# The cumulative sum of the newest gates queued behind the state, and the filling of even slots moved ahead of the output, in a hybrid encoder block

## The chip, the cores and the metric

The kernel runs on one core of a Trainium2 chip. The metric is the device time in microseconds of one execution. Three runs of the kernel before took 1623.01 to 1624.67 us, median 1623.91.

A core has a matrix engine (TensorE, PE in the profile), a vector engine (VectorE, DVE), a scalar engine for activation functions (ScalarE, ACT), an engine that issues most DMAs (SyncE, SP), and GpSimd (POOL), which is hardly used here. Matmuls write to PSUM; DVE and ACT read it out into SBUF. Each engine works through its own queue in order and waits on semaphores for the others.

## The reference

One layer of an encoder over 1024 tokens of width 1024, in float32. The part that matters here is the gated linear attention with 4 heads, keys of 128, values of 256, in both directions:

```
h = RMSNorm(x);  q, k, v, r, gate codes, ... = split(h @ W_in)
log_g = max(log_sigmoid(codes @ up + bias) / 16, -0.5)
b = cumsum(log_g) within a chunk                 # _gla_direction
q_dec = q * exp(b); k_inv = k * exp(-b); k_tail = k * exp(b_last - b)
scores = where(mask, q_dec @ k_inv^T, 0)
o = scores @ v + q_dec @ state
state = exp(b_last) * state + k_tail^T v         # from chunk to chunk
```

The forward direction includes the diagonal, the backward one does not. The two outputs are added, normed per head, gated, and projected. Beside it stands a windowed softmax attention (8 query heads, 2 key heads, window 128), then the merge of the two with an output projection, and a SwiGLU feed-forward.

## The kernel before, in words

Each float32 operand of a matmul is split into a high part (fp32r) made by ACT and a rest made by DVE, and `mm3` (L75) multiplies high by high, high by low and low by high. So every loaded weight of 128x512 costs one ACT copy (`wh`, L67) and one DVE subtraction (`wl`, L69).

The kernel is written with a layer that orders the instructions of DVE, ACT and SP by itself, from the order in the program and its own estimate of when each is ready. Only for PE the written order is kept (`tc.manual_schedule`). Once ordered, each queue is fixed.

The linear attention works in chunks of 128 tokens, NC = 8 for each of NH = 4 heads, 32 in all, as a pipeline over slots `t`. In slot `t` these stages are due (the loop that fills `at` and `behind`):

- `g_gates` for a pair of chunks, in even slots 0 to 30: a matmul of the gate codes into PSUM (`z`), ACT Exp (L419), DVE min (L420), ACT Ln (L421), the DVE scan over 128x512 that makes the cumulative sum (L422), and two small DVE operations for `sm`, the sums at the ends of half chunks (L425, L426). All of it lives in one tile `G`, which has a single buffer.
- `g_decays` (L437 to L444), traced as the last thing of the same even slot: DVE differences, two ACT Exp (L440, L441), and two DVE products with k and q (L443, L444). `g_parts` one slot later splits the results for the matmuls (L451 to L456).
- `g_scores`, three slots after the gates, in odd slots: v is loaded and split (L467, L468), the keys turned on PE and split (L475, L476), the scores computed, read out by ACT into `sp` (L483), masked by DVE (L484) and split into `sh` and `sl` (L487, L488).
- `g_out` for chunk n in slot n + 4, so in every slot from 4 to 35: six matmuls `kv` for the state in both directions; DVE makes the new state `pf` (L502; L506 in a head's first chunk); ACT copies the backward half to `kb` (L504); ACT makes `th`, the high part of the decayed state (L514), and DVE the rest `tl` (L515). Then PE does the output `o`: three matmuls of `sh`, `sl` with v, and three of q with the `th` and `tl` that the *previous* `g_out` made. ACT copies `o` out of PSUM into `ob` (L522).
- `g_back_out`, from slot 12 on in every slot: the backward output (three matmuls with `thb`, `tlb`, L533 and L534), added to `ob` by DVE (L544), and the step of the backward state (`kb`, L536). `g_turn`, twice in each odd slot from 15 on: two transposes and a copy.

Even slots of the steady state thus have the stages gates, back output, output; odd slots have turn, turn, back output, output, scores. Between the stages `slot` (L274) puts filling: matmuls of 128x512 of the other projections, `share(GF, t)` of them in a slot (34 up to slot 7, 21 up to 23, 18 up to 35, then 11). Of `n` fillings and `s` stages, `n * (j + 1) // s` are done after stage `j`, so an equal share stands behind each stage, the last one included. Stages are separate items of the list `work`, and `g_decays` is added to the last of them. `x_sums` adds one or two DVE operations a slot (L576, L581).

All small PSUM tiles of these stages (`z`, `kv`, `o`, the back output, the turned tiles, the scores) share four buffers with the tag `ch`; a tile waits until the one four before it has been read. The tiles `vh`, `kth`, `sh` and their like have one buffer, `th`, `tl` and `pf` two.

Of the kernel before, what the change touches and what calls it, by code (L numbers as in the profile page):

```python
# [8 lines left out]
F32 = mybir.dt.float32  # L9
FR = mybir.dt.float32r  # L10
U32 = mybir.dt.uint32
AF = mybir.ActivationFunctionType
ALU = mybir.AluOpType
# [6 lines left out]
NC = 8  # L20
# [3 lines left out]
GF = ((8, 34), (24, 21), (36, 18), (1 << 30, 11))  # L24
# [6 lines left out]
def body(tc, i, out):  # L31
    nc = tc.nc
    with ExitStack() as root:
# [233 lines left out]
        def share(plan, t):  # L267
            return next(n for end, n in plan if t < end)

        def need(key):  # L270
            while key not in scr:
                fill(12)

        def slot(stages, n):  # L274

            stages = [f for f in stages if f]
            done = 0
            if not stages:
                fill(n)
            for j, f in enumerate(stages):  # L280
                f()
                t = n * (j + 1) // len(stages)
                fill(t - done)
                done = t

# [109 lines left out]
            pass  # L395

        gla = {}

        def g_gates(hd, c):


            pr = Chunk()
            for j in range(2):
                a = gla[hd, c + j] = Chunk()
                a.pr, a.j, a.t = pr, j, slice(j * P, (j + 1) * P)
            s, co = c // 4, (c % 4) * P
            for nme in ("q", "k"):
                need((f"{nme}{hd}", s))
            qk = gtile("qk", (P, 2, 256))
            nc.sync.dma_start(out=qk[:, 0], in_=scr[f"q{hd}", s][:, co:co + 256])  # L410
            nc.sync.dma_start(out=qk[:, 1], in_=scr[f"k{hd}", s][:, co:co + 256])
            z = chtile((P, 2, 256))
            for d in range(2):
                mm(z[:, d], upS[:, d, hd * P:(hd + 1) * P], lrS[:, c * P:(c + 2) * P], True, True)
            G = gtile("G", (P, 4, 2, P), bufs=1)
            Gt = G.rearrange("p a j t -> p a (j t)")
            Gf = G.rearrange("p a j t -> p (a j t)")
            cs, e, csf, ef = G[:, 0:2], G[:, 2:4], Gf[:, 0:512], Gf[:, 512:1024]
            nc.scalar.activation(ef, z.rearrange("p d t -> p (d t)"), AF.Exp, scale=-1.0)  # L419
            nc.vector.tensor_scalar(ef, ef, float(np.expm1(8.0)), None, op0=ALU.min)  # L420
            nc.scalar.activation(ef, ef, AF.Ln, bias=ones[:, 0:1])  # L421
            nc.vector.tensor_tensor_scan(csf, mask.rearrange("p c t -> p (c t)"), ef, 0.0, op0=ALU.mult, op1=ALU.add)  # L422

            pr.sm = gtile("sm", (P, 2, 2, 2), bufs=16)
            nc.vector.tensor_scalar(pr.sm, cs[:, :, :, 63:128:64], -1.0 / 16, None, op0=ALU.mult)  # L425
            nc.vector.tensor_tensor(pr.sm[:, :, :, 1], pr.sm[:, :, :, 1], pr.sm[:, :, :, 0], op=ALU.subtract)  # L426

            pr.qk, pr.G = qk, G

        def g_decays(hd, c):  # L430
            pr = gla[hd, c].pr
            qk, G = pr.qk, pr.G
            Gt = G.rearrange("p a j t -> p a (j t)")
            Gf = G.rearrange("p a j t -> p (a j t)")
            cs, e, csf, ef = G[:, 0:2], G[:, 2:4], Gf[:, 0:512], Gf[:, 512:1024]
            late = bass.AP(Gf.tensor, Gf.offset, [list(Gf.ap[0]), [255, 2], [P, 2], [1, P]])
            nc.vector.tensor_tensor(e, late, cs[:, :, :, 63:64].to_broadcast([P, 2, 2, P]), op=ALU.subtract)  # L437
            nc.vector.tensor_scalar(e[:, 1, :, 0:1], cs[:, 1, :, 63:64], -1.0, None, op0=ALU.mult)

            nc.scalar.activation(csf, ef, AF.Exp, scale=-1.0 / 16)  # L440
            nc.scalar.activation(ef, ef, AF.Exp, scale=1.0 / 16)  # L441
            pr.en = gtile("en", (P, 2, 256))
            nc.vector.tensor_tensor(pr.en, Gt[:, 1:3], qk[:, 1:2].to_broadcast([P, 2, 256]), op=ALU.mult)  # L443
            nc.vector.tensor_tensor(Gt[:, 0:4:3], Gt[:, 0:4:3], qk[:, 0:1].to_broadcast([P, 2, 256]), op=ALU.mult)  # L444
# [48 lines left out]
        def g_out(hd, c):  # L493

            a = gla[hd, c]
            kv = chtile((P, 2, 256))
            for d in range(2):
                mm3(kv[:, d], a.kth[:, d], a.ktl[:, d], a.vh, a.vl, True, True)
            a.pf = gtile("pf")
            if c:  # L500
                pf, dec, th, tl = a.before
                nc.vector.scalar_tensor_tensor(a.pf, pf, dec[:, 0:1], kv[:, 0], op0=ALU.mult, op1=ALU.add)  # L502
                a.kb = gtile(f"kb{c}", bufs=2 if c < 5 else 1)
                nc.scalar.copy(a.kb, kv[:, 1])  # L504
            else:
                nc.vector.tensor_copy(a.pf, kv[:, 0])  # L506
                a.kb = None
            if c < NC - 1:
                n = gla[hd, c + 1]
                dec2 = gtile("dec", (P, 1))  # L510
                nc.scalar.activation(dec2, n.pr.sm[:, 0, n.j, 0:1], AF.Exp, bias=a.pr.sm[:, 0, a.j, 1:2])
                th2 = gtile("th", dt=FR)
                tl2 = gtile("tl", dt=FR)
                nc.scalar.activation(th2, a.pf, AF.Copy, scale=dec2[:, 0:1])  # L514
                nc.vector.scalar_tensor_tensor(tl2, a.pf, dec2[:, 0:1], th2.bitcast(F32), op0=ALU.mult, op1=ALU.subtract)  # L515
                n.before = a.pf, dec2, th2, tl2
            o = chtile((P, 256))
            mm3(o, a.sh, a.sl, a.vh, a.vl, True, c == 0)
            if c:
                mm3(o, a.pr.q2[0][:, 0, a.t], a.pr.q2[0][:, 1, a.t], th, tl, False, True)  # L520
            a.ob = gtile(f"ob{c}", bufs=2 if c < 5 else 1)
            nc.scalar.copy(a.ob, o)  # L522

        def g_back(hd, c):

# [84 lines left out]
        at, behind = {}, {}  # L610
        last = 0
        for n in range(NH * NC):
            hd, c = divmod(n, NC)
            cb = hd * NC + NC + 4 + (NC - 1 - c)
            tt = cb + c % 2 + 2
            for j, (t, f) in enumerate(((n, g_gates), (n + 3, g_scores), (n + 4, g_out),
# [3 lines left out]
                last = max(last, t)  # L620
# [4 lines left out]
        with tc.manual_schedule(engines={mybir.EngineType.PE}):  # L625
            fill(36)
            for t in range(last + 1):
                work = [[at[t, j]] for j in (0, 5, 4, 3, 2, 1) if (t, j) in at]
                if t in behind:
                    work = work or [[]]  # L630
                    work[-1].append(behind[t])
                slot([lambda v=v: [f(*a) for f, *a in v] for v in work], share(GF, t))
                if t:
                    next(sums, None)
        glas.close()
# [186 lines left out]
        for n in range(2 * KT):  # L822
            t, g = divmod(n, 2)
# [9 lines left out]
        order = (prep, a_rope, a_scores, a_turn, k_turn, a_out, a_probs)  # L833
# [165 lines left out]
        with tc.manual_schedule(engines={mybir.EngineType.PE}):  # L999
# [15 lines left out]
            for j in range(0, len(PAIRS), 2):  # L1015
# [4 lines left out]
                v = [pair_T3(f) for f in two]  # L1020
# [561 lines left out]
```

## Time and profile before

| | |
|---|---|
| median of three runs | 1623.91 us |
| the profiled execution | 1624.31 us |
| its span, first to last instruction | 1622.5 us |
| granted TensorE clock | 1.00 throughout |
| busy share of DVE and ACT over the span | 75% and 56% |
| first Exp of the gates (L419) to last copy of a turn (L565) | 49.1 to 368.4 us |

The profile is one execution. Times are in microseconds from the span's start. A row of the timeline has the start, the duration, the engine, the line of the kernel, the operation, the tile written and the tiles read, and in brackets how long the engine sat idle before it and what ended that. Matmuls are pipelined: the duration of one is longer than the step to the next, so PE's pace is read from starts. In the names, `ch` is a small PSUM tile, `mm` one of the filling's; `ch<-vh,kth` is a product for the state, `ch<-vh,sh` one of scores with v, `ch<-th,q2f` one of q with the state.

### The profile page before, as it was taken

The page shows a single profiled execution, that of the slowest core. Times are in us where ns is not written, and L with a number is a line of the kernel's source. Part 1 is how long each engine was busy: PE and PEld are TensorE (multiplying, and loading weights), DVE is VectorE, ACT ScalarE, POOL GpSimd, SP SyncE. Part 2 cuts the span into 40 slices and gives each one's busy share as a digit, 9 for nine tenths or more (in the row PEclk, how much of TensorE's full clock was granted, in tenths as well). Part 3 has the DMA queues.
Part 4 walks back from the last instruction along what each step waited for, and adds up shares of the span by engine and source line. Part 5 has one row for each costly group of instructions (what it writes and reads, how often), then busy time and mean ns, then how long its engine had stood idle before and what let it go on. Part 6 is the DMA issues. An engine that isn't in the chain of part 4 may idle for free.

```text
span 1622.5 us, 23392 instructions
## 1 busy us (share of the span) xinstructions
PE 1611.6 (99%) x7644; PEld 1341.5 (83%) x7644; DVE 1223.9 (75%) x2315; ACT 915.0 (56%) x1883; POOL 0.2 (0%) x4
## 2 busy tenths in 40 slices
PE   9999999999999999999999999999999999999999
PEld 7888888888888888888888888888888888888887
DVE  8568888845999777876855878677777888789655
ACT  7456777873999745445732547754444444354442
POOL 0000000000000000000000000000000000000000
PEclk9999999999999999999999999999999999999999
DMA  8855757878554487878842656643435564695433
GB/s 279 295 180 194 252 172 256 274 264 284 176 162 143 129 268 253 270 242 263 282 126 89 192 192 214 196 141 124 136 121 177 170 219 146 207 328 189 149 98 117
DMA packets 196362, 323.25 MB, mean 199 GB/s; under 512 B 22318, under 2 KB 47790, under 8 KB 196240
## 3 DMA queue, kind: packets, MB, share of 16 engines
q1 hardware_dynamic: 196240, 321.76, 60.8%
q8 instruction: 60, 0.98, 0.2%
q14 instruction: 62, 0.51, 0.1%
HBM read 216.29 MB, written 105.38 MB: 198 GB/s over the span
## 4 chain that ended last, share of the span: by engine, by line
PE 89%; DVE 4%; ACT 3%; DMA 2%; issue 1%; SPq 0%; DVEq 0%; ACTq 0%
PE mm L73 20%; PE mm L877 10%; PE mm L879 10%; PE mm L878 10%; PE mm L1421 7%; PE ch L73 7%; PE ch L1421 6%; PE ch L878 5%; PE ch L879 5%; PE ch L877 5%; PE mm L246 3%; PE ch L783 1%; DMA kvr<-skv 1%; DMA st<-in_xT_dram 1%; DVE wl L69 0%
## 5 line engine op out<-in xcount | busy, mean ns | idle before, releaser
L856 ACT ACTIVATE wh<-ws 128x512 fp32r<-128x512 f32 x164 | 102.9, 629 | 152.5 <-PE mm L878 81.0
L73 PE MATMUL mm<-wh,xh 128*128 128x512 f32 x320 | 127.1, 397 | 0.0
L73 PE MATMUL mm<-wh,xl 128*128 128x512 f32 x320 | 127.1, 397 | 0.0
L73 PE MATMUL mm<-wl,xh 128*128 128x512 f32 x320 | 126.6, 395 | 0.0
L857 DVE TENSOR_TENSOR wl<-ws,wh 128x512 fp32r<-128x512 f32 x164 | 112.2, 686 | 14.0 <-ACT wh L856 13.5
L67 ACT ACTIVATE wh<-wr 128x512 fp32r<-128x512 f32 x118 | 73.5, 627 | 53.0 <-PE mm L73 21.3
L69 DVE TENSOR_TENSOR wl<-wr,wh 128x512 fp32r<-128x512 f32 x118 | 80.8, 686 | 25.2 <-ACT wh L67 22.8
L856 ACT ACTIVATE wh<-a 128x512 fp32r<-128x512 f32 x66 | 41.6, 632 | 89.1 <-PE ch L1421 42.3
L856 ACT ACTIVATE wh<-wr 128x512 fp32r<-128x512 f32 x76 | 47.8, 631 | 58.1 <-PE mm L878 17.6
L857 DVE TENSOR_TENSOR wl<-a,wh 128x512 fp32r<-128x512 f32 x66 | 45.5, 690 | 39.7 <-ACT wh L856 39.3
L1421 PE MATMUL mm<-hh,wl 128*128 128x512 f32 x176 | 68.6, 390 | 0.0
L1421 PE MATMUL mm<-hl,wh 128*128 128x512 f32 x176 | 68.5, 389 | 0.0
L1421 PE MATMUL mm<-hh,wh 128*128 128x512 f32 x176 | 68.5, 389 | 0.0
L73 PEld LDWEIGHTS mm<-wl,xh 128*128 128x128 f32 x320 | 60.2, 188 | 9.8
L73 PEld LDWEIGHTS mm<-wh,xl 128*128 128x128 f32 x320 | 60.2, 188 | 9.6
L73 PEld LDWEIGHTS mm<-wh,xh 128*128 128x128 f32 x320 | 60.3, 188 | 9.1 <-DVE st L141 0.2
L857 DVE TENSOR_TENSOR wl<-wr,wh 128x512 fp32r<-128x512 f32 x76 | 52.0, 685 | 7.8 <-ACT wh L856 7.1
L870 DVE TENSOR_TENSOR ws<-wr,wr 128x512 f32<-128x512 f32 x80 | 54.5, 687 | 4.3 <-DMA wr<-in_w_f_dram 1.7
L1388 DVE TENSOR_TENSOR hl<-hr,hh 128x512 fp32r<-128x512 f32 x77 | 52.8, 686 | 5.7 <-ACT hh L1387 5.4
L1387 ACT ACTIVATE hh<-hr 128x512 fp32r<-128x512 f32 x77 | 47.7, 619 | 9.0 <-DMA hr<-B 5.1
L1421 PE MATMUL ch<-hh,wh 128*128 128x512 f32 x132 | 51.3, 389 | 0.0
L1421 PE MATMUL ch<-hl,wh 128*128 128x512 f32 x132 | 51.3, 389 | 0.0
(454 smaller groups left out, 4984.5 us busy)
## 6 DMA issues: line engine op xcount, KB each, us to landing
wr<-in_w_fi_dram SPq DMA_DIRECT2D x110, 256.0 KB, 3.9
wr<-in_w_f_dram SPq DMA_DIRECT2D x100, 256.0 KB, 3.7
wh<-wh SPq DMA_DIRECT2D x80, 256.0 KB, 3.1
wl<-wl SPq DMA_DIRECT2D x80, 256.0 KB, 3.1
B<-c SPq DMA_DIRECT2D x44, 256.0 KB, 2.1
T<-st SPq DMA_DIRECT2D x44, 256.0 KB, 2.9
a<-in_w_fo_dram SPq DMA_DIRECT2D x44, 256.0 KB, 5.3
hr<-T SPq DMA_DIRECT2D x44, 256.0 KB, 2.7
```

The costliest lines, as they stand in the source:

```text
L67: nc.scalar.activation(h, raw, AF.Copy)
L69: nc.vector.tensor_tensor(l, raw, h.bitcast(F32), op=ALU.subtract)
L73: nc.tensor.matmul(o, a, b, start=start, stop=stop)
L246: nc.tensor.matmul(Y[q], w[:, c], x, start=f0, stop=f1, skip_group_check=True)
L856: nc.scalar.activation(h, src, AF.Copy)
L857: nc.vector.tensor_tensor(l, src, h.bitcast(F32), op=ALU.subtract)
L870: nc.vector.tensor_tensor(t, x, y, op=op)
L877: nc.tensor.matmul(o, h[:, c], x[kk][0], start=start and kk == 0, stop=False, skip_group_check=True)
L878: nc.tensor.matmul(o, h[:, c], x[kk][1], start=False, stop=False, skip_group_check=True)
L879: nc.tensor.matmul(o, l[:, c], x[kk][0], start=False, stop=kk == nk - 1, skip_group_check=True)
L1388: nc.vector.tensor_tensor(l, r, h.bitcast(F32), op=ALU.subtract)
L1421: nc.tensor.matmul(ys[m], a[:, c], b, start=f0, stop=f1, skip_group_check=True)
```

## The change

Three functions are touched.

1. The scan and the two `sm` operations move from the end of `g_gates` to the start of what was `g_decays`, now `g_sums`. `g_decays` traces all of `g_sums` in `tc.issue_after(v)` for each `v` in the list `state`: every instruction in the block is queued behind `v` on `v`'s engine. `state` holds `th`'s ACT instruction and `tl`'s DVE instruction of the last `g_out` that made them. In an even slot `g_out` is traced just ahead of `g_decays`, so these are the same slot's. Before slot 4 the list is empty.
2. `g_out` notes these two instructions.
3. `slot` takes a flag. Where it is false and there is more than one stage, the `n` fillings are spread behind all stages but the last, none behind the last. It is false in even slots that have an output (4 to 34).

The number of instructions and of fillings in a slot stays.

```diff
-        def slot(stages, n):
+        def slot(stages, n, last=True):
...
-                t = n * (j + 1) // len(stages)
+                t = n * (j + 1) // len(stages) if last or len(stages) == 1 else n * min(j + 1, len(stages) - 1) // (len(stages) - 1)
...
         gla = {}
+        state = []
...
             nc.scalar.activation(ef, ef, AF.Ln, bias=ones[:, 0:1])
-            nc.vector.tensor_tensor_scan(csf, mask.rearrange("p c t -> p (c t)"), ef, 0.0, op0=ALU.mult, op1=ALU.add)
-
-            pr.sm = gtile("sm", (P, 2, 2, 2), bufs=16)
-            nc.vector.tensor_scalar(pr.sm, cs[:, :, :, 63:128:64], -1.0 / 16, None, op0=ALU.mult)
-            nc.vector.tensor_tensor(pr.sm[:, :, :, 1], pr.sm[:, :, :, 1], pr.sm[:, :, :, 0], op=ALU.subtract)
-
             pr.qk, pr.G = qk, G
 
         def g_decays(hd, c):
-            pr = gla[hd, c].pr
+            with ExitStack() as order:
+                for v in state:
+                    order.enter_context(tc.issue_after(v.ins))
+                g_sums(gla[hd, c].pr)
+
+        def g_sums(pr):
             qk, G = pr.qk, pr.G
...
+            nc.vector.tensor_tensor_scan(csf, mask.rearrange("p c t -> p (c t)"), ef, 0.0, op0=ALU.mult, op1=ALU.add)
+
+            pr.sm = gtile("sm", (P, 2, 2, 2), bufs=16)
+            nc.vector.tensor_scalar(pr.sm, cs[:, :, :, 63:128:64], -1.0 / 16, None, op0=ALU.mult)
+            nc.vector.tensor_tensor(pr.sm[:, :, :, 1], pr.sm[:, :, :, 1], pr.sm[:, :, :, 0], op=ALU.subtract)
+
             late = bass.AP(Gf.tensor, Gf.offset, [list(Gf.ap[0]), [255, 2], [P, 2], [1, P]])
...
-                nc.scalar.activation(th2, a.pf, AF.Copy, scale=dec2[:, 0:1])
-                nc.vector.scalar_tensor_tensor(tl2, a.pf, dec2[:, 0:1], th2.bitcast(F32), op0=ALU.mult, op1=ALU.subtract)
+                v1 = nc.scalar.activation(th2, a.pf, AF.Copy, scale=dec2[:, 0:1])
+                v2 = nc.vector.scalar_tensor_tensor(tl2, a.pf, dec2[:, 0:1], th2.bitcast(F32), op0=ALU.mult, op1=ALU.subtract)
...
             nc.scalar.copy(a.ob, o)
+            if c < NC - 1:
+                state[:] = v1, v2
...
-                slot([lambda v=v: [f(*a) for f, *a in v] for v in work], share(GF, t))
+                slot([lambda v=v: [f(*a) for f, *a in v] for v in work], share(GF, t), t % 2 == 1 or (t, 2) not in at)
```

More of the change, by code (lines that the diff above doesn't have):

```diff
@@ L421, in g_gates, with g_decays @@
             nc.scalar.activation(ef, ef, AF.Ln, bias=ones[:, 0:1])
+            pr.qk, pr.G = qk, G
+        def g_decays(hd, c):
+            with ExitStack() as order:
[3 more added lines that the diff above has]
+        def g_sums(pr):
+            qk, G = pr.qk, pr.G
+            Gt = G.rearrange("p a j t -> p a (j t)")
+            Gf = G.rearrange("p a j t -> p (a j t)")
+            cs, e, csf, ef = G[:, 0:2], G[:, 2:4], Gf[:, 0:512], Gf[:, 512:1024]
             nc.vector.tensor_tensor_scan(csf, mask.rearrange("p c t -> p (c t)"), ef, 0.0, op0=ALU.mult, op1=ALU.add)
```

6 lines of the change are left out of this document (removed).

## The prediction

> **What bounds the kernel now.** I read the page first: TensorE (PE) is busy all the time, and the chain that ended last is PE for 89% of the span. So only two things can move the time: idle of PE that goes, and idle that comes.
>
> ```profile
> PE 1611.6 (99%) x7644; PEld 1341.5 (83%) x7644; DVE 1223.9 (75%) x2315; ACT 915.0 (56%) x1883; POOL 0.2 (0%) x4
> ```
>
> Next came the table of busy time by stretch. Its columns are the stretch, its length, then busy time and instruction count of PE, weight loads (PEld), DVE and ACT. The slots of the linear attention fill the first quarter of the span. Its slots 4 to 11 lie in the first row below; slots 28 to 31 lie in the rows from 270 to 315.
>
> ```profile
> 75.00:145.00 70.00, 70.00 (x381) 60.38 (x380) 50.13 (x100) 35.75 (x79) 0.00 (x0) 1.00 0.58 191
> 270.00:285.00 15.00, 15.00 (x91) 13.13 (x90) 13.30 (x33) 11.45 (x35) 0.00 (x0) 1.00 0.74 229
> 285.00:300.00 15.00, 13.66 (x83) 11.43 (x82) 13.15 (x32) 12.83 (x34) 0.00 (x0) 1.00 0.86 295
> 300.00:315.00 15.00, 15.00 (x93) 13.16 (x92) 14.33 (x35) 12.87 (x37) 0.00 (x0) 1.00 0.84 283
> 740.00:1100.00 360.00, 359.38 (x1585) 297.20 (x1584) 259.37 (x414) 196.99 (x338) 0.00 (x0) 1.00 0.59 186
> ```
>
> Three things are to be seen. The early slots have no idle PE at all (70.00 of 70.00). The last pairs of slots lose some, and there DVE is nearly full (14.33 of 15). And a 512-wide matmul takes PE 360/1585 = 0.23 us from start to start where nothing waits, although its row says 0.39; so a wait has to be read from the starts. The view of the waits of PE names what it waited for in the attention (total, times, longest):
>
> ```profile
> PE ch L73 <- ACT ob L522: 1.4, 2, 1.1
> PE ch L73 <- DVE sh L487: 0.8, 2, 0.6
> PE ch L73 <- DVE sl L488: 0.2, 1, 0.2
> ```
>
> That is 2.4 us of idle in five places. PE's timeline at these five places, from start to start:
>
> ```profile
> 217.40 0.28 PE L73 MATMUL ch<-vl,sh 128*128 128x256 f32 x1
> 217.84 0.39 PE L73 MATMUL ch<-vh,sl 128*128 128x256 f32 x1 [0.16 <-DVE sl L488]
> ...
> 224.03 0.28 PE L73 MATMUL ch<-vh,ktl 128*128 128x256 f32 x1
> 224.64 0.38 PE L73 MATMUL ch<-vh,sh 128*128 128x256 f32 x1 [0.33 <-ACT ob L522]
> ...
> 285.73 0.28 PE L73 MATMUL ch<-vh,ktl 128*128 128x256 f32 x1
> 286.27 0.36 PE L73 MATMUL ch<-vh,sh 128*128 128x256 f32 x1 [0.26 <-DVE sh L487]
> 286.86 0.40 PE L73 MATMUL mm<-wh,xl 128*128 128x512 f32 x1
> ...
> 291.14 0.40 PE L73 MATMUL mm<-wh,xl 128*128 128x512 f32 x1
> 292.62 0.39 PE L73 MATMUL ch<-vh,kth 128*128 128x256 f32 x1 [1.08 <-ACT ob L522]
> ...
> 315.22 0.28 PE L73 MATMUL ch<-vh,ktl 128*128 128x256 f32 x1
> 316.07 0.36 PE L73 MATMUL ch<-vh,sh 128*128 128x256 f32 x1 [0.57 <-DVE sh L487]
> ```
>
> The normal step of a 256-wide matmul is 0.12 us (next fence: 106.31 to 106.43). Above the normal step the five places lose 0.32, 0.49, 0.42, 1.25 and 0.73 us, 3.2 together. Behind a wait the next matmuls are slow too: from 286.27 to 286.86 three of them take 0.59 where 0.36 is normal, 0.23 more. With 0.1 to 0.23 behind four of them, I count **3.9 us** as all that this stage can give back. Against the span that is 0.24%.
>
> What makes them wait is order on DVE and ACT. The longest one, on those engines' timelines (slot 28, an even one):
>
> ```profile
> 287.71 1.22 DVE L422 TENSOR_TENSOR_SCAN G<-mask,G 128x512 f32<-128x512 f32 x1 [0.79 <-ACT G L421]
> 289.05 0.68 DVE L437 TENSOR_TENSOR G<-G 128x512 f32<-128x512 f32 x1
> 289.73 0.42 DVE L506 COPY pf<-ch 128x256 f32<-128x256 f32 x1
> ...
> 290.18 0.51 ACT L514 ACTIVATE th<-pf,dec 128x256 fp32r<-128x256 f32 x1 [1.41 <-DVE pf L506]
> 292.20 0.36 ACT L522 COPY ob<-ch 128x256 f32<-128x256 f32 x1
> ```
>
> The products for the state ended at about 286 (285.73 + 0.28), yet `pf` starts at 289.73, because the newest gates' scan and L437 were put in front of it. ACT stood idle 1.41 us for `pf`; the copy of the output out of PSUM (L522) is behind that in ACT's queue, and PE needed the PSUM buffer that it frees.
>
> **The change part by part.**
>
> *The scan behind the state.* No instruction is added; the scan, the two `sm` operations, and the whole of `g_decays` (DVE L437 to L444, ACT L440 and L441) come behind `th` and `tl` of the same slot's `g_out`. That takes 1.22 + 0.68 us and the small ones, about 2 us, from in front of `pf`. Queued behind the new order are only these operations themselves. Their readers are `g_parts` one slot later and `g_scores` three slots later, and the next pair's Exp into the single buffer G two slots later, so being some 3 us late costs nothing by my count. What hides this is DVE's free time late in the odd slot and early in the even slot; without it the readers are late, see the second rival. No DMA is moved by this and no SP queue passed. The next late thing is `pf` itself, behind the state's matmuls.
>
> *No filling behind the output in even slots.* The number of dense matmuls in a slot stays, so no matmul is added. In slots of three stages a third of the filling (7 of 21, 6 of 18, at 0.23 us each: 1.6 or 1.4 us) goes from behind the output to in front of it. So the scores (`sh`, `sl`) of the slot before have that much more time before an even `g_out` needs them; three of the five waits are such, and none had more than 0.73 us. The other two (`ob`) wait behind `pf` in an even slot. All five lie in the reach of one half or the other: **minus 3.9 us**, and I take half of it, 2 us, as the weak end.
>
> What it costs: the next `g_out`, in the odd slot, comes sooner. From slot 14 on two turns, a back output and 8 to 12 fillings lie between. Slot 14 of before:
>
> ```profile
> 170.08 0.28 PE L73 MATMUL ch<-vh,ktl 128*128 128x256 f32 x1
> ...
> 177.19 0.28 PE L73 MATMUL ch<-th,q2f 128*128 128x256 f32 x1
> ```
>
> From the last product for the state to the first matmul that reads it are 7.1 us, and 7.1 - 1.6 = 5.5 after the change. Slots 4, 6, 8 and 10 are another matter. They have two stages (gates; output), so all filling goes in front of the output; and the odd slots behind them begin with their own `g_out`, as no turn and no back output exists yet. There **two outputs now stand back to back**. How long does PE need from the one's last product to the matmul that reads its `tl`, and how long does the state need? Rows of slot 6 and slot 8 (PE, DVE, ACT):
>
> ```profile
> 106.31 0.28 PE L73 MATMUL ch<-vh,ktl 128*128 128x256 f32 x1
> 106.43 0.28 PE L73 MATMUL ch<-vh,sh 128*128 128x256 f32 x1
> ...
> 106.63 0.48 DVE L502 SCALAR_TENSOR_TENSOR pf<-pf,dec,ch 128x256 f32<-128x256 f32 x1 [0.41 <-PE ch L73]
> ...
> 126.38 0.47 DVE L502 SCALAR_TENSOR_TENSOR pf<-pf,dec,ch 128x256 f32<-128x256 f32 x1
> 126.89 0.37 ACT L504 COPY kb<-ch 128x256 f32<-128x256 f32 x1 [0.34 <-DVE pf L502]
> 127.15 0.51 ACT L514 ACTIVATE th<-pf,dec 128x256 fp32r<-128x256 f32 x1
> 127.70 0.48 DVE L515 SCALAR_TENSOR_TENSOR tl<-pf,dec,th 128x256 fp32r<-128x256 f32 x1 [0.77 <-ACT th L514]
> ```
>
> PE: six matmuls of the first output, six products, three of `sh`, then `th` and `tl`: the 17th matmul, 17 x 0.12 = 2.04 us (14 x 0.12 = 1.68 in slot 4, whose output has three matmuls). The state with free engines: 106.63 - 106.31 = 0.32 to the start of `pf`, then 127.70 + 0.48 - 126.38 = 1.80 to the end of `tl`, 2.12 us. So it is late by 0.08 us at the least, and with the slow restart 0.1 to 0.3. The other end is slot 10, where the scan and a weight's split stood in the way:
>
> ```profile
> 139.70 0.28 PE L73 MATMUL ch<-vh,ktl 128*128 128x256 f32 x1
> ...
> 143.12 0.48 DVE L515 SCALAR_TENSOR_TENSOR tl<-pf,dec,th 128x256 fp32r<-128x256 f32 x1
> ```
>
> 143.60 - 139.70 = 3.9 us, late by 1.86, with the restart 2.1. The lower end is the nearer row, since the scan is now behind the state; but DVE and ACT still take a split of a weight now and then (0.69 us on DVE, by the page's row), just ahead of `pf` or `th`:
>
> ```profile
> L69 DVE TENSOR_TENSOR wl<-wr,wh 128x512 fp32r<-128x512 f32 x118 | 80.8, 686 | 25.2 <-ACT wh L67 22.8
> ```
>
> I take **0.6 us a pair, four pairs: plus 2.4 us**, ends 0.4 and 8.4. A gain is excluded there: no idle exists in that stretch. The sum of filling before slot 4 and behind slot 36 is untouched.
>
> Sum: -3.9 + 2.4 + 0.2 for a wait somewhere that I don't see = **-1.3 us**. The profiled execution took 1624.31 us (span 1622.5, 1.8 around it), 0.4 above the median 1623.91; it would become 1623.0, and the median **1622.6**.
>
> A rule to weigh: the PE column of the stretch from 285 to 300 loses 15 - 13.66 = 1.34 us, whereas the starts say 0.42 + 0.23 + 1.25 + 0.1 = 2.0. The Trainium skill, Perfetto Trace Analysis, section Identifying the Most-Contended Engine, says that matmul busy time is a poor measure and that the busy share of weight loads is a good one. By that share this stretch does 11.43 where the one before does 13.13 of 15, (13.13 - 11.43)/0.875 = 1.9 us lost, so the rule sides with the starts; going by the matmul column alone the gain would be 2.4 and the sum +0.2.
>
> **The rivals.** Measurements of this kernel can tell about 0.2%, 3.2 us, from no change; that is the bound for "faster" and "slower".
>
> *Paid in the close pairs (slower).* The state between two outputs that stand back to back takes about as long as in slot 10. Then four pairs pay up to 2.1 us each, 8.4 - 3.9 = +4.5: 1628.4. It decides from 1.8 us a pair on, that is from a state of 3.6 us. For it: slot 10's row, and that DVE and ACT serve queues in order, so any split in front counts in full. Against: most of the 3.9 us is the scan and L437, which the change itself moves.
>
> *The backlog moves (same).* In the late slots DVE is nearly full, and what is held behind the state falls into the odd slot, ahead of the scores' `sp`, `sh`, `sl`. Slot 31 of before:
>
> ```profile
> 315.16 0.44 DVE L484 COPY_PREDICATED sp<-tri,ch 128x256 f32<-128x256 uint32 x1
> 315.63 0.29 DVE L487 CAST sh<-sp 128x256 fp32r<-128x256 f32 x1
> ```
>
> If `sh` comes later by the 2 us of the scan's group and PE asks for it 1.4 us later, each of some four such waits of 0.6 us stays, 2.4 of the 3.9 us are kept as loss, and the sum is -1.5 + 2.4 + 0.2 = +1.1: 1625.0. For it: 14.33 of 15. Against: in the even slot DVE now has 4 us of filling in which no scan comes.
>
> *Nothing paid (faster).* The five waits go and the pairs cost 0.4: -3.5, 1620.4, just beyond the bound. Needs DVE and ACT free at four moments. That the change has no effect at all is excluded only for the filling, which is PE's written order; that the scan was behind the state in most slots anyway is a part of "same".
>
> **How the numbers follow.** Forecast (five waits mostly gone, pairs at about 0.6): 0.55. Backlog: 0.15. Close pairs dear: 0.16. Nothing paid: 0.14. Faster is the last alone, 0.14; slower the close pairs, 0.16; within 0.2% the rest, 0.70. The range reaches from all gain and no price, 1620.2, to half the gain (2 us) with 1.3 us a pair (5.2), +3.2, 1627.1. I give 1620.2 to 1627.0.
>
> **What would show it.** In the profile after: no PE wait for `ob` or `sh` between 210 and 320 us; `pf` within 0.5 us of the last product in even slots, and the scan behind `tl`; in the stretch from 75 to 145 us four short waits of PE for DVE `tl` or ACT `th`, 0.1 to 0.6 us each. Wrong would be: waits of over 1.5 us there; waits for `sh` in even slots that stay or grow; a wait of ACT's Exp (L419) for DVE L456, which would say that G's single buffer has become the bound; or a difference that lies behind the linear attention, where I expect none.

## The result and the profile after

The changed kernel takes 1628.69 us (median of nine runs, 1627.69 to 1629.91), the kernel before 1624.35 us (nine runs, 1622.91 to 1626.17). The ratio is 1.0028, with a 95% interval of 1.0020 to 1.0037: slower by 4.3 us, where 1622.6 was forecast and 1627.0 was the upper end. The profiled execution after took 1627.69 us with a span of 1625.9 us, 3.4 us more than the span of before. It is the quickest of the nine, so the trace shows a little less than the medians do.

The page's row of engines, after. PE still fills the span, so the loss is idle PE again:

```profile
PE 1613.3 (99%) x7644; PEld 1341.7 (83%) x7644; DVE 1218.9 (75%) x2315; ACT 915.8 (56%) x1883; POOL 0.2 (0%) x4
```

The table of busy time by stretch (stretch, length, then PE, PEld, DVE and ACT), first one row of before that the prediction does not have, then rows of after:

```profile
75.00:330.00 255.00, 252.59 (x1446) 217.90 (x1445) 207.02 (x463) 177.64 (x467) 0.00 (x0) 1.00 0.68 223
```

```profile
75.00:330.00 255.00, 250.77 (x1426) 214.71 (x1424) 199.27 (x454) 174.13 (x457) 0.00 (x0) 1.00 0.67 219
740.00:1100.00 360.00, 360.00 (x1589) 297.84 (x1588) 258.86 (x414) 196.54 (x337) 0.00 (x0) 1.00 0.59 189
```

From 75 to 330 us, the slots of the linear attention, after has done 20 matmuls fewer in the same time, and its weight loads are 217.90 - 214.71 = 3.2 us behind; at 217.90/255 = 0.85 of busy time that is 3.7 us. From 740 to 1100 us it does as much as before (360.00 against 359.38). So the loss lies in the linear attention. DVE does not do more there but less (199.27 against 207.02): it is late, not overfull.

What PE waited for from 60 us on, after, as far as it lies in the attention (total, times, longest):

```profile
PE mm L73 <- DVE st L141: 1.4, 1, 1.4
PE ch L73 <- ACT kb L510: 1.0, 1, 1.0
...
PE ch L73 <- DVE pf L512: 0.6, 1, 0.6
...
PE ch L73 <- DVE tl L521: 0.4, 1, 0.4
...
PE ch L73 <- DVE sl L494: 0.3, 1, 0.3
...
PE ch L73 <- DVE ob L552: 0.2, 1, 0.2
```

The waits for `ob` L522 and `sh` L487 are gone at all five places that the prediction listed; at two of them (slots 28 and 32) PE now waits for `sl`, 0.14 and 0.44 us from start to start. Other names stand at new places. The timeline of PE at four of these:

```profile
91.24 0.34 PE L73 MATMUL ch<-th,q2f 128*128 128x256 f32 x1
92.01 0.38 PE L73 MATMUL ch<-tl,q2f 128*128 128x256 f32 x1 [0.43 <-DVE tl L521]
...
153.05 0.40 PE L73 MATMUL mm<-wh,xl 128*128 128x512 f32 x1
154.84 0.50 PE L73 MATMUL mm<-wh,xh 128*128 128x512 f32 x1 [1.39 <-DVE st L141]
...
291.71 0.40 PE L73 MATMUL mm<-wh,xl 128*128 128x512 f32 x1
292.76 0.39 PE L73 MATMUL ch<-thb,q2b 128*128 128x256 f32 x1 [0.65 <-DVE pf L512]
...
323.40 0.39 PE L73 MATMUL mm<-wh,xl 128*128 128x512 f32 x1
324.74 0.39 PE L73 MATMUL ch<-thb,q2b 128*128 128x256 f32 x1 [0.96 <-ACT kb L510]
```

From start to start, above the normal step of 0.12 us (256 wide) or 0.23 us (512 wide), these lose 0.65, 1.56, 0.82 and 1.11 us. Behind most waits the next step is slow as well, by 0.10 or 0.11 us, as the prediction counted it too. What is to be explained can be read without any normal step: from the first product of the gate codes to the last turn, PE runs the same matmuls in 319.75 us before (48.33 to 368.07) and in 323.91 us after, 4.2 us more. The losses from the starts:

| what PE waits for | waiting steps | with the slow step behind each |
|---|---|---|
| pairs of outputs back to back (slots 4 to 11): 0.65, 0.15, 0.15, 0.15 | 1.1 us | 1.5 us |
| slot 12: a dense product, for the PSUM buffer that `st` (L141) reads | 1.6 us | 1.7 us |
| back outputs of odd slots, for the PSUM buffer of `kv` (`pf`, `kb`), six times from 224 to 325 us | 2.7 us | 3.4 us |
| `sl` L494 (three times) and `ob` L552 (twice) | 1.4 us | 1.7 us |
| the five waits of before | -3.2 us | -3.9 us |

With the slow steps that is +4.4 us, about the 4.2 of the whole stretch.

Why is `st` late? DVE in slot 10, after, then the same operations before:

```profile
143.31 0.48 DVE L508 SCALAR_TENSOR_TENSOR pf<-pf,dec,ch 128x256 f32<-128x256 f32 x1 [1.73 <-PE ch L73]
144.64 0.48 DVE L521 SCALAR_TENSOR_TENSOR tl<-pf,dec,th 128x256 fp32r<-128x256 f32 x1 [0.85 <-ACT th L520]
145.04 1.22 DVE L436 TENSOR_TENSOR_SCAN G<-mask,G 128x512 f32<-128x512 f32 x1
...
152.30 0.68 DVE L458 TENSOR_TENSOR kl<-en,kh 128x512 fp32r<-128x512 f32 x1
...
153.77 0.42 DVE L462 TENSOR_TENSOR q2b<-G,q2b 128x256 fp32r<-128x256 f32 x1
154.10 1.28 DVE L141 TENSOR_TENSOR st<-mm,rstd 128x512 f32<-128x512 f32 x2
```

```profile
139.44 1.23 DVE L422 TENSOR_TENSOR_SCAN G<-mask,G 128x512 f32<-128x512 f32 x1 [0.79 <-ACT G L421]
...
147.25 0.42 DVE L456 TENSOR_TENSOR q2b<-G,q2b 128x256 fp32r<-128x256 f32 x1
...
151.45 0.68 DVE L141 TENSOR_TENSOR st<-mm,rstd 128x512 f32<-128x512 f32 x1
```

The order is what the change says: `pf` starts 0.04 us after PE's last product for the state (142.99 + 0.28), and the scan comes behind `tl`. But DVE stands idle for 1.73 us in front of `pf` and 0.85 us in front of `tl`, with the scan in its queue behind them. (Its input, the Ln on ACT, had ended at 141.74, so it was ready for some 1.5 of these 1.73 us.) The scan starts 5.6 us later than before, the parts made from it (`kl`, `q2b`) 6.5 us later, and so they now fall in front of `st`, which comes 2.65 us later. Idle of DVE in front of `pf`, from 75 to 330 us, before and after:

```profile
DVE pf L502 <- PE ch L73: 0.4, 1, 0.4
DVE pf L506 <- PE ch L73: 0.4, 1, 0.4
```

```profile
DVE pf L508 <- PE ch L73: 10.0, 8, 3.6
...
DVE pf L512 <- PE ch L73: 2.1, 2, 2.0
```

e2_fill below has the changed kernel's order on PE and no hold; there DVE's idle in front of `pf` is 0.6 us. So the 12.1 us come from the hold.

### The profile page after: what moved, and what is told of

Same layout as the page of the kernel before. It is cut to its first block, busy times and chain, and to the rows that moved or that the text cites. A ratio compares the mean times of both kernels' runs of the same rounds, so it can differ in the third digit from the quotient of the medians.

```text
span 1625.9 us, 23421 instructions
## 1 busy us (share of the span) xinstructions
PE 1613.3 (99%) x7644; PEld 1341.7 (83%) x7644; DVE 1218.9 (75%) x2315; ACT 915.8 (56%) x1883; POOL 0.2 (0%) x4
## 4 chain that ended last, share of the span: by engine, by line
PE 87%; DVE 5%; ACT 4%; DMA 2%; issue 1%; SPq 0%; DVEq 0%; ACTq 0%
PE mm L73 17%; PE mm L885 10%; PE mm L887 10%; PE mm L886 10%; PE mm L1429 7%; PE ch L73 6%; PE ch L1429 6%; PE ch L887 5%; PE ch L885 5%; PE ch L886 5%; PE mm L246 3%; PE ch L791 1%; ACT p L774 1%; ACT p L780 1%; DMA kvr<-skv 1%
## 5 line engine op out<-in xcount | busy, mean ns | idle before, releaser
L1429 PE MATMUL ch<-hh,wl 128*128 128x512 f32 x132 | 51.4, 389 | 0.0
```

Of the source, the lines that this page charges most:

```text
L1429: nc.tensor.matmul(ys[m], a[:, c], b, start=f0, stop=f1, skip_group_check=True)
```

## The experiments

Two explanations stood against each other: that the loss comes from the hold (scan and decays queued behind the state, so that DVE waits with work in hand), or that it comes from the filling (products and outputs at other times, so that outputs stand close and PSUM buffers are asked for sooner). All numbers are medians against runs of the kernel before on the same chip (1623.5 to 1623.9 us), with the ratio and its 95% interval.

### Each half alone: e1_scan and e2_fill

e1_scan is the change with the old filling:

```diff
-                slot([lambda v=v: [f(*a) for f, *a in v] for v in work], share(GF, t), t % 2 == 1 or (t, 2) not in at)
+                slot([lambda v=v: [f(*a) for f, *a in v] for v in work], share(GF, t))
```

> The scan and the decays behind the state, with the filling left as before. PE's order is that of the kernel before. Theory F (the loss comes from the filling taken away behind the even output, because the back output and the next output then ask sooner for what the state frees): no loss, 0 to 2 us faster than before, and no wait of PE for kb or pf at the back output. Theory S (the loss comes from the scan and the decays being late, which pushes DVE's other work into the odd slot): most of the loss is here, 3 to 4 us slower than before, with the 1.4 us wait for the read-out of a dense product (st) and a wait for sl still there.

1631.30 us, +7.8, ratio 1.0051 (1.0039 to 1.0064), about twice what the second theory foresaw. Its waits of PE, the two longest:

```profile
PE mm L73 <- DVE st L141: 2.8, 1, 2.8
PE ch L73 <- DVE sh L493: 2.3, 3, 1.8
```

Not all of the 7.8 us is waiting. In the trace the TensorE clock is at half for 3.4 us behind the wait for `sh` (see the end), which by 3.4 x 0.5 costs about 1.7 us, an estimate; the whole executions have a granted clock of 0.998 or 0.999, those of the change but one 1.000.

e2_fill has only the new filling: the scan, `sm` and decays stand where they stood before (the edit against the change, cut).

```diff
             nc.scalar.activation(ef, ef, AF.Ln, bias=ones[:, 0:1])
+            nc.vector.tensor_tensor_scan(csf, mask.rearrange("p c t -> p (c t)"), ef, 0.0, op0=ALU.mult, op1=ALU.add)
...
-            with ExitStack() as order:
-                for v in state:
-                    order.enter_context(tc.issue_after(v.ins))
-                g_sums(gla[hd, c].pr)
...
```

> Only the filling moved ahead of the even output; scan and decays ordered as before. Theory F: 3 to 6 us slower than before, with waits at the back output of odd slots, and the four close pairs of outputs dearer than the 1.1 us that they cost after the change, since the scan can again stand in front of the state. Theory S: 0 to 2 us faster than before, as the scores' waits go.

1628.68 us, +5.2, ratio 1.0034 (1.0021 to 1.0048). Its waits of PE, the three longest:

```profile
PE ch L73 <- ACT th L514: 2.4, 3, 1.0
PE ch L73 <- DVE tl L515: 2.0, 5, 0.7
PE ch L73 <- ACT kb L504: 1.9, 2, 1.0
```

The hold alone costs more than both together (+4.3); the filling alone costs about as much, for the two intervals overlap. Without the hold the four close pairs cost 5.7 us in their waiting steps (1.0 more in slots 12 and 13), with it 1.1. It is not the scan that stands in front of `pf` in those slots of e2_fill, for it is done before the state's products; the decays' products, the parts made from them and other work are there. In slot 8:

```profile
129.94 0.69 DVE L443 TENSOR_TENSOR en<-G,qk 128x512 f32<-128x512 f32 x1 [1.42 <-ACT G L441]
130.55 0.69 DVE L444 TENSOR_TENSOR G<-G,qk 128x512 f32<-128x512 f32 x1
131.15 0.47 DVE L502 SCALAR_TENSOR_TENSOR pf<-pf,dec,ch 128x256 f32<-128x256 f32 x1
```

The state's products had ended at 129.90 (129.62 + 0.28). Without the filling `sh` is late by up to 1.84 us, and with it that wait is gone. So the two halves do repair each other's damage, but each brings some that the other does not repair: the hold brings `st` (2.8 us alone, 1.4 with the filling), the filling brings the wait for `kb` (1.9 us in e2_fill, which has no hold).

### The pairs: e3_late and e4_lead

e3_late leaves the filling behind the output in slots before 14, so that no two outputs stand back to back.

```diff
-                slot([lambda v=v: [f(*a) for f, *a in v] for v in work], share(GF, t), t % 2 == 1 or (t, 2) not in at)
+                slot([lambda v=v: [f(*a) for f, *a in v] for v in work], share(GF, t), t % 2 == 1 or (t, 2) not in at or t < 14)
```

> The change, but even slots before 14 keep the filling behind their output, so no two outputs stand back to back. Both theories: the waits for tl at the pairs go, 1.1 us by the gaps of the trace after, so about 1 us faster than the changed kernel and still 2 to 3 us slower than before. If the pairs cost more than the trace shows, the time falls nearer to before.

1630.55 us, +7.1, ratio 1.0043 (1.0030 to 1.0055): a miss. The pairs' waits went but for one of 0.40 us, yet the loss for `st` grew from 1.56 to 2.97 us, as in e1_scan (2.97). With filling behind the output the product that wants the buffer comes sooner, and DVE is no sooner. The profiled execution, at a granted clock of 1.000, took 1629.14 us; the other four, at 0.998 or 0.999, took 1630.51 us and more, so part of the median is clock.

e4_lead keeps the change, and in odd slots behind an even slot with an output puts the last share of the filling ahead of the first stage. So the filling stands between the two outputs and ahead of the back output, and none stands behind the scores.

```diff
-        def slot(stages, n, last=True):
+        def slot(stages, n, last=True, lead=False):
...
+            if lead and len(stages) > 1:
+                m = n - n * (len(stages) - 1) // len(stages)
+                fill(m)
+                for j, f in enumerate(stages):
+                    f()
+                    t = n * min(j + 1, len(stages) - 1) // len(stages)
+                    fill(t - done)
+                    done = t
+                return
...
-                slot([lambda v=v: [f(*a) for f, *a in v] for v in work], share(GF, t), t % 2 == 1 or (t, 2) not in at)
+                slot([lambda v=v: [f(*a) for f, *a in v] for v in work], share(GF, t), t % 2 == 1 or (t, 2) not in at, t % 2 == 1 and (t - 1, 2) in at)
```

> The change, with the share of filling that stands behind the last stage of an odd slot put in front of its first stage, so that 4 to 17 fillings stand again between an even output and what follows it, and none behind the scores. Theory F: the waits at the back output and at the pairs go, 0 to 2 us faster than before. Theory S: the waits for st and sl stay, 2 to 3 us slower than before.

1625.96 us, +2.5, ratio 1.0018 (1.0009 to 1.0026). There is no wait left for a pair or for `st`, and the stretch from the first product of the gate codes to the last turn takes 320.51 us, 0.8 more than before. Waits for `kb` (1.8 us in 2) and `ob` (1.3 in 2) stay in the attention. The rest of the loss is behind it, in the softmax attention, with one wait of 1.42 us for `pl` and a lower clock after it (see the end).

### The late parts in front of the read-out: e5_parts, e11_before_parts

If the parts ahead of `st` make it late, then tracing them behind the odd slot's last filling must take that wait away, with the hold still in place.

```diff
-                if t in behind:
+                if t in behind and t % 2 == 0:
                     work = work or [[]]
...
+                if t in behind and t % 2:
+                    f, *v = behind[t]
+                    f(*v)
```

> The change, with g_parts traced behind the last filling of its odd slot, so that its DVE and ACT operations come behind the read-out of a dense product that ends in that filling. PE's order is the same. If the 1.4 us wait for st in slot 12 comes from decays and parts that are late and stand in front of it in DVE's queue (1.3 us of parts are in front of it), that wait falls to 0.4 us or less and the time by about 1 us against the changed kernel. If st is late for another reason (its own matmuls, or the cumulative work of the slot), the wait stays.

1626.77 us, +3.1, ratio 1.0022 (1.0013 to 1.0031). The scan is as late as in after (145.12), but `st` is back at 152.37 and the parts follow at 154.09. `st` is gone from the list of PE's waits in the attention, and the others stay as after (`kb` 1.0 us, `pf` 0.6). The gain on the change, 1.2 us, has the size of the 1.7 lost there, although the two intervals overlap; the trace decides. On the kernel before, the same edit does nothing:

> The kernel before with parts traced behind the last filling of their slot. Before had no wait for st, and parts were done before it; the waits for sh in even slots (0.26 and 0.57 us) may shrink. Within 1 us of before; over 2 us slower would mean that parts are needed sooner than I count.

1624.23 us, ratio 1.0003 (0.9994 to 1.0011). There the parts are early and hinder nobody.

### The PSUM buffer of `kv`: e6_turn, e7_both, e8_before_turn

The `ch` tiles take four buffers in turn, so the back output of an odd slot (behind two turns) waits for the readers of `kv` of the even slot. With both turns in one tile and one copy, it waits for another. The copy in SBUF then has one buffer where it had two, and its four DMAs leave together.

```diff
+        turned = []
...
-            ot = chtile((P, 2, P))
+            if c % 2:
+                turned[:] = [chtile((P, 2, 2, P))]
+            ot = turned[0]
             for j in range(2):
-                nc.tensor.transpose(ot[:, j], a.ob[:, j * P:(j + 1) * P], ident)
+                nc.tensor.transpose(ot[:, c % 2, j], a.ob[:, j * P:(j + 1) * P], ident)
+            if c % 2:
+                return
-            os_ = gtile("ot", (P, 2, P))
+            os_ = gtile("ot", (P, 2, 2, P), bufs=1)
             nc.scalar.copy(os_, ot)
...
```

> The change, with the two turns of an odd slot in one PSUM tile and one ACT copy, so the stages take ten small PSUM buffers in a pair of slots and not eleven, and the back output of an odd slot takes the place of the even slot's back output, not that of the products kv. PE's order is the same. If the waits at the back output (0.65 and 0.96 us named for pf and kb, and five small ones, some 3 us by the gaps) come from the buffer of kv, they go, 2 to 3 us faster than the changed kernel. If they come from the data of the back output, they stay.

1628.75 us, +5.1, ratio 1.0034 (1.0021 to 1.0046). The longest of its waits of PE (`st` has 1.4 us, as in the change):

```profile
PE ch L73 <- DVE ob L552: 1.7, 3, 0.7
```

Every wait at the back output is gone, so it was the buffer of `kv`. But the scores, the next in the ring, now wait for the back output's own reader, `ob` L552: nothing gained. In a ring of four, a tile fewer moves the wait to the next tile while the readers are as late as before.

> The change with both mends, parts behind the last filling and one tile for two turns. If both causes are right, 3 to 4 us faster than the changed kernel, that is within 1.5 us of before.

e7_both has e5's and e6's edits: 1626.89 us, +3.3, ratio 1.0020 (1.0011 to 1.0029), e5_parts over again.

> The kernel before with the two turns of an odd slot in one PSUM tile. Its waits for ob are waits for the same four buffers; if only the buffer counts, the two ob waits (1.8 us by the gaps) go and the kernel is 1 to 2 us faster than before. If the engines' order behind them counts, another wait takes their place and nothing changes.

On the kernel before, the turn's edit gives 1623.55 us, ratio 1.0001 (0.9992 to 1.0010). The waits for `ob` L522 fall from 1.4 to 0.6 us in the trace, but the time does not follow.

### How much must be held: e9_scanfree, e13_dvehold, e14_acthold

e9_scanfree is the change with the scan and `sm` outside the hold; only the decays stay behind the state.

```diff
         def g_decays(hd, c):
...
+            nc.vector.tensor_tensor_scan(csf, mask.rearrange("p c t -> p (c t)"), ef, 0.0, op0=ALU.mult, op1=ALU.add)
...
             with ExitStack() as order:
                 for v in state:
                     order.enter_context(tc.issue_after(v.ins))
-                g_sums(gla[hd, c].pr)
+                g_sums(pr)
...
-            nc.vector.tensor_tensor_scan(csf, mask.rearrange("p c t -> p (c t)"), ef, 0.0, op0=ALU.mult, op1=ALU.add)
...
```

> The change with the scan and the two sm operations left free to go before the state; the decays (differences, Exps, products) stay behind it, and the filling stays moved. PE's order is that of the changed kernel. Theory H (the hold leaves DVE idle in front of pf, 10 us in 8 waits, while the scan is ready, and that work is late afterwards): the idle of DVE in front of pf falls, the wait for st shrinks from 1.4 us, 1 to 2 us faster than the changed kernel. Theory N (the scan in front of pf is what hurts, the hold is right): pf is late again, the close pairs cost more than 1.1 us and the waits at the back output grow, 1 to 3 us slower than the changed kernel.

1627.97 us, +4.0, ratio 1.0025 (1.0016 to 1.0034), not to be told from the change. DVE's idle in front of `pf` L511 fell from 10.0 to 5.0 us (L515 has 2.0 more, as in the change) and the wait for `st` went, but the waits at the back output grew from 1.6 to 4.5 us:

```profile
PE ch L73 <- ACT kb L513: 2.9, 3, 1.3
PE ch L73 <- DVE pf L515: 1.6, 2, 1.4
```

So it does not tell what the scan's share is. It does tell what keeps the close pairs cheap: they lose 0.65, 0.15, 0.15 and 0.15 us as in the change, with the scan free, so there it is enough to hold the decays. e13_dvehold and e14_acthold split the hold by engine instead, both with the old filling (as e1_scan): the first holds DVE's operations alone, behind `tl`, the second ACT's alone, behind `th`.

```diff
-                for v in state:
+                for v in state[1:]:
```

> Scan and decays behind tl on DVE alone, the Exps on ACT free, filling as before; to be compared with the kernel that holds both (7.8 us over before). Theory H (DVE's idle in front of pf is the loss): the Exps need the scan, so they are behind tl anyway: 6 to 8 us over before, with the waits for st in slot 12 and for sh in slot 32 still there. If ACT's order is the loss: 0 to 2 us over before.

1631.46 us, +7.6, ratio 1.0046 (1.0033 to 1.0058). Its waits of PE:

```profile
PE mm L73 <- DVE st L141: 2.6, 1, 2.6
PE ch L73 <- DVE sh L493: 2.3, 3, 1.9
```

```diff
-                for v in state:
+                for v in state[:1]:
```

> Only the Exps of the decays behind th on ACT; on DVE scan and decays are free, filling as before. Theory H: the Exps came behind th or close to it before as well, so within 1.5 us of before. If ACT's order is the loss: 4 us or more over before.

1623.30 us, -0.6, ratio 0.9998 (0.9989 to 1.0007), with waits of PE as before the change, `ob` first:

```profile
PE ch L73 <- ACT ob L528: 1.3, 2, 1.0
```

So the price of the hold (7.8 us in e1_scan) comes with DVE's order. As in e1_scan, a part of it is clock: e13_dvehold has granted clocks of 0.997 to 0.999, and its trace has two stretches of 3.4 us at half clock. Holding ACT's two Exps costs nothing that can be measured.

### A better filling without the hold: e10_lead_parts, e12_before_lead, e15_lead_turn

e10_lead_parts is e4's filling with e5's parts.

> The kernel with the odd slots' last filling put in front (some 2.5 us over before), with parts traced behind the last filling as well. Its trace had no wait for st, so parts have little to give: within 1 us of it. If it is 1 to 2 us faster, parts were in the way of something else too.

1625.73 us, +1.8, ratio 1.0013 (1.0005 to 1.0022): as e4_lead, which had no wait for `st` left to mend.

e12_before_lead has the filling of e4_lead on the kernel before, so PE's order is that of e4_lead, and nothing is held.

> Scan and decays as before, filling as in the kernel whose odd slots' last share stands in front. If the filling behind the scores is what the waits for sh lack nothing of, and the hold is the rest of the loss (theory H), this is the best of the moved fillings: between 1.5 us faster than before and 1 us slower. If it is slower than the kernel with the hold (2.5 us over before), the hold helps once the filling is moved.

1620.88 us, -3.1, ratio 0.9980 (0.9971 to 0.9989): it beats both kernels. Its waits of PE in the attention are two short ones:

```profile
PE ch L73 <- ACT kb L513: 0.4, 1, 0.4
PE ch L73 <- ACT ob L531: 0.3, 1, 0.3
```

From the first product of the gate codes to the last turn it takes 316.87 us, 2.9 less than before: most of the 3.9 that the prediction counted as to be had. e4_lead, the same with the hold, is 5.5 us slower against its own runs of before (+2.5 and -3.1). In the two traces 3.6 us of that lie in this stretch (320.51 against 316.87); the rest lies behind it. e10_lead_parts, measured beside e12_before_lead, has the hold and no lowered clock in its trace, and is 4.9 us slower.

> The fastest kernel so far (filling ahead of the even output, odd slots' last share in front, no hold; 3 us under before) with one PSUM tile for the two turns. Its waits for kb and ob are waits for these buffers, 0.9 us by the gaps; if they go and nothing comes in their place, 0.5 to 1 us faster; as in the other kernels with this edit, a wait of the scores for ob may take their place, and then the time is the same within 0.5 us.

With one tile for both turns as well: 1620.73 us, ratio 0.9980 (0.9971 to 0.9989). No more is to be had from that ring.

## Why the prediction was wrong

- **The five waits, "minus 3.9 us": right.** All five are gone, with 0.14 and 0.44 us for `sl` in the place of two, and e12_before_lead, which pays no new wait of weight for them, shows that a gain of that kind is there (-3.1 us).
- **The pairs, "0.6 us a pair, four pairs: plus 2.4 us": the right kind, too dear.** The four take 1.1 us, and 1.5 with the slow step behind each. The state took what the nearer row said: in slot 10 from 142.99 to the end of `tl` at 145.12, 2.13 us where 2.12 was counted. The hold of the decays does its work here: in e2_fill, without it, the four cost 5.7 us. The rival in which close pairs are dear named nearly the measured time (1628.4) for a cause that is not there.
- **"Being some 3 us late costs nothing by my count": this step failed.** It counted the direct readers of the scan, which have slack, and not what the held work pushes away. DVE serves its queue in order: in slot 10 it stood idle for 1.73 us with the ready scan behind `pf`. What is held behind `tl` does not fill the time until PE delivers the state's products, so that time (0.8 us before, 12.1 after) is idle, and the same operations are done later, ahead of somebody else's: `st`, and in e1_scan `sp` and `sh`. "DVE's free time late in the odd slot and early in the even slot" was the cover named; the part early in the even slot is what the hold spent. In slot 10 the scan was 5.6 us late, not 3. e13_dvehold shows that DVE's order alone carries the price, e5_parts that it is the late parts that delay `st`. The idle itself is not the price: e1_scan has 5.7 us of it and costs 7.8, the change has 12.1 and costs 4.3. What costs is what comes late behind it.
- **A wait of ACT's Exp for `q2b`,** which the prediction named as a sign of being wrong, did appear. Before it stood 0.22 us once; ACT's waits after, 75 to 330 us:

```profile
ACT G L420 <- DVE q2b L462: 6.9, 5, 2.4
```

Late parts make the next pair's gates late through the single buffer G, and those the next scan. The longest of these waits, 2.44 us, ends at 139.50, ahead of slot 10's scan: the Ln there ended 2.3 us later than before (141.74 against 139.41), so only 3.3 of the scan's 5.6 us lie between its input and its start. The bulk of the price does not hang on it, for e1_scan has 0.7 us of such waits. No PE wait was traced to it alone, and a second G was not tried.

- **"`pf` within 0.5 us of the last product in even slots": true in ten of sixteen.** From slot 4 to 18 it starts 0.04 us after that product (in slots 8 to 18 of before 0.95 to 2.81). In slots 20, 22 and 26 to 32 it starts 1.9 to 3.5 us after it, although the scan is behind `tl`: taking the scan's group out of the way was not enough there, since other work stood in front too. The prediction put the late `pf` of slot 28 down to the scan and L437; it was 3.7 us late before and is 2.8 us late without them.
- **"0.2 for a wait somewhere that I don't see": too small by far.** Missed were `st` at 1.7 us, the back output at 3.4 us, and `sl` and `ob` at 1.7 us. For the odd slot the prediction judged the 1.6 us that it moved forward only by the distance from the state's products to `th` ("7.1 - 1.6 = 5.5"); the back output, which stands ahead of that and needs the buffer that `pf` and `kb` free, was not asked. In slot 28 of before, `pf` started at 289.73, 3.7 us after its last product, and nobody waited, because the back output came 4.3 us after that product:

```profile
290.31 0.28 PE L73 MATMUL ch<-thb,q2b 128*128 128x256 f32 x1
```

After the change the products end at 289.16 + 0.28 = 289.44 and `pf` starts 2.85 us later, so it is not later than before; but the back output is due after 2.5 us (292.76 - 0.82 = 291.94). Between the products' end and `pf` DVE does two splits of weights, three operations of the backward state (L544, L542), and stands idle for 0.28 us:

```profile
289.92 0.68 DVE L69 TENSOR_TENSOR wl<-wr,wh 128x512 fp32r<-128x512 f32 x1
...
291.68 0.69 DVE L69 TENSOR_TENSOR wl<-wr,wh 128x512 fp32r<-128x512 f32 x1 [0.28 <-ACT wh L67]
292.29 0.42 DVE L512 COPY pf<-ch 128x256 f32<-128x256 f32 x1
```

These are the same splits that the prediction weighed for the pairs, at another place.

- **The rival "the backlog moves" had the mechanism** (held work falls into the odd slot, ahead of others' work) with too small a price: it kept 2.4 of the old waits for `sh`, and gave 1625.0. Where it bites is `st`, which no wait of PE in before pointed to.
- **No difference behind the linear attention: right for the change** (359.38 and 360.00 us of PE from 740 to 1100). It does not hold for e4_lead, whose loss lies there; why `pl` is late in that kernel is open.

By the sum: -3.9 + 1.5 + 1.7 + 3.4 + 1.7 = +4.4 us in the starts, where -3.9 + 2.4 + 0.2 = -1.3 was forecast.

## What to carry to other kernels

Before you hold ready work behind an instruction that waits for another engine, count the wait: on an engine that serves its queue in order, the held work gets none of that time, and comes out later in front of work that nobody looked at. When a step moves forward, go through everything between its old and its new place, the read-outs of PSUM buffers too, and not only the operand that you had in mind. Test the halves of a paired change apart: here neither was a gain alone, and the better kernel has no hold, keeps the even slots' filling ahead of the output, and puts the odd slots' last share where it stands between the two outputs.

## What the hardware showed that was not expected

A short wait of PE can cost twice. In e1_scan PE waited 1.84 us for `sh`, and the next dense steps took 0.42 us instead of 0.23 (322.06 to 322.48):

```profile
318.45 0.28 PE L73 MATMUL ch<-vh,ktl 128*128 128x256 f32 x1
...
320.57 0.35 PE L73 MATMUL ch<-vh,sh 128*128 128x256 f32 x1 [1.84 <-DVE sh L493]
...
322.06 0.63 PE L73 MATMUL mm<-wh,xl 128*128 128x512 f32 x1
322.48 0.63 PE L73 MATMUL mm<-wh,xh 128*128 128x512 f32 x1
```

The table by stretch has the granted clock third from the right. First e1_scan, just after a wait of 2.80 us for `st` and after this one of 1.84 us:

```profile
155.50:159.00 3.50, 3.11 (x16) 2.69 (x17) 3.07 (x7) 1.06 (x2) 0.00 (x0) 1.00 0.75 286
321.00:324.80 3.80, 3.64 (x12) 3.01 (x12) 2.32 (x5) 1.70 (x6) 0.00 (x0) 0.56 0.70 244
```

Then e4_lead, during and after its wait of 1.42 us for `pl`:

```profile
452.00:454.40 2.40, 0.98 (x5) 0.58 (x5) 1.21 (x3) 2.40 (x6) 0.00 (x0) 0.99 0.90 301
454.40:457.50 3.10, 3.10 (x10) 2.64 (x9) 2.19 (x8) 2.29 (x4) 0.00 (x0) 0.50 0.25 94
```

From 321.00 to 321.40 the clock is still 1.00, from 321.40 to 324.80 it is 0.50. So it was at half for about 3.4 us after waits of 1.42 and 1.84 us, and 1.00 after one of 2.80 us. e10_lead_parts has the wait for `pl` too, of 1.41 us, and its clock stays at 1.00. The length of the wait alone does not decide. The Trainium skill, TensorE: Matmul & The Clock Gate, section What's actually happening, has the array fall back to half rate after at least one idle window of about 3.4 us, counted in windows that run on their own. The two rates and the 3.4 us fit, and a phase that runs on its own would fit the waits that cost nothing. But in e4_lead PE was busy for 1.61 of the 3.41 us up to the drop (450.93 to 454.34): if that was the window, 1.8 us of idle time in it were enough.
